# One weight load for two half-height matmuls: the Gram matrices of a cross-covariance attention kernel

## The chip, the cores and the metric

The kernel runs on one NeuronCore of a Trainium2 chip. The metric is the device time of one execution in microseconds (us), the median of several runs. A second number is used for reading: the span, which is the time from the first to the last instruction in one profiled execution.

## The reference

For each of 8 x 12 = 96 heads, Q, K and V are 512 x 64 in float32. Q and K are normalised along the sequence, a 64 x 64 matrix of attention is made from them, and V is multiplied by it:

```python
Q_norm = Q / (np.linalg.norm(Q, axis=-2, keepdims=True) + 1e-10)
K_norm = K / (np.linalg.norm(K, axis=-2, keepdims=True) + 1e-10)
attn = np.einsum('bhnd,bhne->bhde', Q_norm, K_norm)
attn = np.exp(attn - np.max(attn, axis=-1, keepdims=True))
attn = attn / (np.sum(attn, axis=-1, keepdims=True) + 1e-10)
return np.einsum('bhnd,bhde->bhne', V, attn)
```

## The kernel before

**Units.** Four heads make a unit u; there are U = 24 units. Two units make a step s (12 steps), two steps a window w of V (6 windows). In a unit's tiles each head lies on 32 partitions, and each partition holds T = 16 rows of 64 numbers. So partitions 0 to 63 hold heads 0 and 1, and partitions 64 to 127 hold heads 2 and 3.

**What a unit goes through.** Q and K arrive by DMA and are cast to bf16 into `qkb[u]`, K beside Q (`cast_qk`, on DVE, ACT or POOL). `mask_k` (L222, DVE) writes `km[u]`: K twice, side by side, once with the odd heads set to zero and once with the even heads set to zero. `square_q` (L228, ACT) squares Q. Then TensorE (PE) has four kinds of work and a fifth for V:

- `grams(u)` (L245): for each of 16 rows t and for each half g of the partitions, a matmul with 64 rows of `km` as weights (64 x 128) and the same 64 partitions of `qkb` as moving data (128 columns, K and Q). It accumulates K'K and K'Q of two heads in PSUM tile `gram`, each half g in a bank of its own. This makes 32 matmuls and 32 weight loads in a unit, 768 of each in all.
- `norms_q(u)` (L253): 8 matmuls with full-height weights and 4 columns of moving data, for the norms of Q.
- `logits(s)` (L300): two float32 transposes for a step.
- `vtrans` (L327): transposes of V, in groups of 8 (4 at the end), full-height weights.
- `outs(s, x)` (L343): 16 matmuls with weights of 128 x 32, the product of V and attention.

Between them stand `squares`, `cross`, `halves_q`, `sums`, `powers`, `scale_k`, `exps` and `normalise` (DVE, ACT, POOL) for the softmax, and the copies out of PSUM, `vcopy` and `ocopy`. Results leave by DMA on the queue of SP.

**What sets the order.** The order on each engine is written out by a planner (class `Order`): every piece of work has costs on its engines, pieces that it must follow and a rank, and a list simulation gives each engine's sequence. `grams` has a cost of 1.8 us for the first eight units and 1.2 us after; `size` counts PE instructions of a piece (64 for a `grams`), and `pause` stands for the fetching of PE's code. None of these numbers is changed. `km` and `qkb` have two buffers each, so that the casts of unit u + 2 wait for the Gram matmuls of unit u. PE executes in the order written, so that whatever stands behind a `grams` waits for it.

The profile calls a weight load LDWEIGHTS, on a row of its own, PEld. It names PE's instructions with the rows and columns of the array that they use: 64\*128 for the Gram matmuls and their loads, 128\*128 for `norms_q`, `logits` and `vtrans`, 128\*32 for `outs`.

## Time and profile before

| | |
|---|---|
| median of 3 runs | 127.69 us (127.62 to 127.79) |
| span of the profiled execution | 125.9 us |
| the profiled execution's own time | not listed beside its span; median less span is 1.8 us |
| mean granted clock of TensorE | 0.870 of full speed |
| PE busy / PEld busy | 79.6 us / 63.9 us |
| DVE / ACT / POOL busy | 98.8 / 91.0 / 50.0 us |
| moved by DMA | 50.63 MB, mean 402 GB/s |
| Gram matmuls (L245) | 768, mean 252 ns, 33.3 us busy |
| Gram weight loads (L245) | 768, mean 113 ns, 28.3 us busy |

Matmuls and loads are pipelined, so that the ends in the records are modelled, and records of neighbours overlap: 768 matmuls of 252 ns take 33.3 us and not 194. The starts are events. "Idle before, releaser" gives the time that an engine stood idle ahead of a group of instructions, and who ended that idleness.

### The profile page before, as it was taken

How to read it: one execution, taken by the hardware profiler on the slowest of the kernel's cores; microseconds unless marked ns; L12 is line 12 of the kernel's file. 1: busy time of each engine (PE TensorE's matmuls, PEld its weight loads, DVE VectorE, ACT ScalarE, POOL GpSimd, SP SyncE). 2: the span in 40 equal slices, each digit the busy share in tenths (PEclk: the TensorE clock that was granted, in tenths of full speed). 3: DMA queues.
4: the chain of work that ended last, by engine and by line, in shares of the span. 5: the costliest groups of instructions: out<-in, count | busy, mean ns of one | idle time of the engine just before them, and what ended most of it. 6: DMA issues, size and time to landing. Idle time of an engine off the chain costs nothing.

```text
span 125.9 us, 4630 instructions
## 1 busy us (share of the span) xinstructions
PE 79.6 (63%) x1944; PEld 63.9 (51%) x1944; DVE 98.8 (78%) x198; ACT 91.0 (72%) x217; POOL 50.0 (40%) x68
## 2 busy tenths in 40 slices
PE   0036949258789857766776668676794875976000
PEld 0035848236668745555665555555683764754000
DVE  3189676967959399987999989999979999999200
ACT  4243476579979999499999999999499997670000
POOL 6243353384561836633437226138743551000000
PEclk9999999955555899999999999999779999599555
DMA  3999999999999999999999999999999999999993
GB/s 105 401 419 419 422 414 418 432 424 410 439 409 418 414 433 414 410 431 419 411 428 428 403 419 423 424 424 407 426 413 420 410 415 407 417 411 404 400 411 134
DMA packets 12159, 50.63 MB, mean 402 GB/s; under 512 B 1130, under 2 KB 1130, under 8 KB 10730
## 3 DMA queue, kind: packets, MB, share of 16 engines
q1 hardware_dynamic: 11850, 49.29, 95.9%
q10 hardware_dynamic: 288, 1.05, 2.1%
q8 instruction: 15, 0.25, 0.7%
q14 instruction: 6, 0.05, 0.1%
HBM read 37.75 MB, written 12.58 MB: 400 GB/s over the span
## 4 chain that ended last, share of the span: by engine, by line
DVE 32%; ACT 24%; DMA 18%; PE 8%; issue 7%; POOL 3%; ACTq 0%; SPq 0%; POOLq 0%
DMA out_dram<-so 12%; DVE so L174 12%; DVE km L222 10%; DMA qk<-in_K_dram 6%; PE gram L245 6%; ACT vt L172 5%; ACT q L228 5%; ACT qkb L172 4%; ACT ex L307 4%; DVE ab L316 4%; DVE qkb L174 3%; ACT vb L172 2%; ACT kq L172 2%; POOL vb L176 2%; DVE n L280 1%
## 5 line engine op out<-in xcount | busy, mean ns | idle before, releaser
L245 PE MATMUL gram<-qkb,km 64*128 64x128 bf16 x768 | 33.3, 252 | 23.3 <-DVE km L222 23.3
L245 PEld LDWEIGHTS <-km 64*128 64x128 bf16 x768 | 28.3, 113 | 26.7 <-DVE km L222 26.3
L176 POOL TENSOR_SCALAR qkb<-qk 128x1024 bf16<-128x1024 f32 x24 | 25.4, 1062 | 28.6 <-PE gram L245 19.9
L222 DVE TENSOR_SCALAR km<-qkb,pick 128x1024 bf16<-128x1024 bf16 x48 | 30.3, 671 | 3.0 <-ACT qkb L172 2.4
L174 DVE COPY so<-po 128x512 f32<-128x512 f32 x48 | 30.8, 684 | 0.4
L228 ACT ACTIVATE q<-qk 128x1024 bf16<-128x1024 f32 x24 | 25.5, 1065 | 6.3 <-DMA qk<-in_Q_dram 4.3
L343 PE MATMUL po<-ab,vt 128*32 128x128 bf16 x768 | 20.1, 231 | 9.5 <-DVE so L174 6.9
L172 ACT COPY vt<-vps 128x1024 bf16<-128x1024 bf16 (+1 forms) x26 | 24.5, 956 | 1.2 <-PE vps L327 1.0
L343 PEld LDWEIGHTS <-vt 128*32 128x32 bf16 x768 | 13.4, 100 | 14.9 <-issue 10.7
L327 PE MATMUL vps<-identb,vb 128*128 128x128 bf16 x192 | 16.7, 237 | 3.0 <-ACT vt L172 2.2
L176 POOL TENSOR_SCALAR vb<-v 128x1024 bf16<-128x1024 f32 x13 | 15.0, 1156 | 8.4 <-DMA v<-in_V_dram 8.2
L307 ACT ACTIVATE ex<-lg,r 128x64 f32<-128x64 f32 x48 | 14.5, 325 | 1.6 <-PE lg L300 1.6
L327 PEld LDWEIGHTS <-vb 128*128 128x128 bf16 x192 | 12.6, 106 | 6.0 <-issue 3.1
L174 DVE CAST qkb<-qk 128x1024 bf16<-128x1024 f32 x13 | 12.1, 933 | 4.2 <-DMA qk<-in_K_dram 4.1
L293 POOL TENSOR_TENSOR kqs<-kq,r 128x256 f32<-128x256 f32 x12 | 7.9, 660 | 18.8 <-ACT r L289 8.3
L316 DVE TENSOR_TENSOR ab<-ex,rinv 64x256 bf16<-64x256 f32 x24 | 12.1, 504 | 0.6
L260 DVE SCALAR_TENSOR_TENSOR scr<-gram,eye 128x256 f32<-128x256 f32 x12 | 5.1, 424 | 8.5 <-ACT kq L172 5.7
L172 ACT CAST vb<-v 128x1024 bf16<-128x1024 f32 x11 | 11.7, 1062 | 0.0
L172 ACT CAST qkb<-qk 128x1024 bf16<-128x1024 f32 x11 | 11.6, 1054 | 0.0
L307 ACT ACTIVATION_READ_ACCUMULATOR ex<-lg,r 128x1 f32 x48 | 10.4, 217 | 0.0
L172 ACT COPY kq<-gram 128x256 f32<-128x256 f32 x12 | 4.6, 380 | 7.1 <-PE gram L253 3.1
L253 PEld LDWEIGHTS <-q 128*128 128x128 bf16 x192 | 7.5, 100 | 3.7 <-issue 2.7
(25 smaller groups left out, 41.1 us busy)
## 6 DMA issues: line engine op xcount, KB each, us to landing
out_dram<-so SPq DMA_DIRECT2D x23, 512.0 KB, 9.8
v<-in_V_dram SPq DMA_DIRECT2D x11, 1024.0 KB, 15.8
qk<-in_Q_dram SPq DMA_DIRECT2D x8, 1024.0 KB, 15.9
qk<-in_K_dram SPq DMA_DIRECT2D x8, 1024.0 KB, 17.6
qk<-in_Q_dram SPq DMA_DIRECT2D x8, 512.0 KB, 8.7
qk<-in_K_dram SPq DMA_DIRECT2D x6, 512.0 KB, 9.6
qk<-in_K_dram ACTq DMA_DIRECT2D x2, 512.0 KB
v<-in_V_dram SPq DMA_DIRECT2D x2, 512.0 KB
```

The lines of the kernel that those rows point to most:

```text
L172: nc.scalar.copy(o, i)
L174: nc.vector.tensor_copy(o, i)
L176: nc.gpsimd.tensor_scalar(out=o, in0=i, scalar1=1.0, scalar2=0.0, op0=ALU.mult, op1=ALU.add)
L222: nc.vector.tensor_scalar(out=km[u][:, :, a], in0=qkb[u][:, :, 0], scalar1=pick[:, a:a + 1], scalar2=None, op0=ALU.mult)
L228: nc.scalar.activation(q2[u], qk32[s][:, 0, r], AF.Square)
L245: nc.tensor.matmul(gram[s][:, 2 * g + r, 0:2 * D], km[u][rows, t].rearrange("p a d -> p (a d)"), qkb[u][rows, t].rearrange("p x d -> p (x ...
L253: nc.tensor.matmul(gram[s][:, 0, 2 * D + HU * r:2 * D + HU * (r + 1)], q2[u][:, 2 * t:2 * t + 2].rearrange("p t d -> p (t d)"), heads, sta ...
L293: (nc.vector if eng == "DVE" else nc.gpsimd).tensor_tensor(out=kqs[s], in0=kq[s], in1=r8[s][:, 0:HU, None].to_broadcast([128, 4, D]), op=A ...
L307: nc.scalar.activation(e[:, h, :], lg[s][:, h, :], AF.Exp, scale=r8[s][:, HU + h:HU + h + 1], accum_out=z[:, h:h + 1])
L316: nc.vector.tensor_tensor(out=a[half, :, half], in0=e[half], in1=ri[half, :, None].to_broadcast([D, HU, D]), op=ALU.mult,)
L327: nc.tensor.transpose(ps[:, c, n, :], vb[w][:, J * c + j].rearrange("p r d -> p (r d)"), identb)
L343: nc.tensor.matmul(po[s, x][32 * h:32 * (h + 1), j].rearrange("p r d -> p (r d)"), v, ab[s][:, h, :])
```

## The change

In `grams`, the two matmuls of a row t, one for each half of the partitions, no longer bring a weight load each. One load takes all 128 partitions of `km[u][:, t]`. Two matmuls follow, written by the new helper `stay` as bare matmul instructions that bring no load; each has the array tile of 64 rows and 128 columns at row 0 or row 64, the same moving data and the same place in PSUM as before. So a unit has 16 loads in the place of 32, and 32 matmuls as before. Nothing else is changed, the planner's numbers included.

```diff
+    def stay(o, w, i, size, at, start, stop):
+
+        low = nc.tensor.lower_ap
+        nc.tensor.add_instruction(mybir.InstMatmult(
+            name=nc.get_next_instruction_name(), engine=mybir.EngineType.PE, ins=[low(i), low(w)], outs=[low(o)],
+            start_tensor_calc=start, stop_tensor_calc=stop, tile_size=size, tile_position=at, ldweights=False))
+
...
         for t in range(T):
+            w = km[u][:, t].rearrange("p a d -> p (a d)")
+            nc.tensor.ldweights(w)
             for g in range(2):
                 rows = slice(64 * g, 64 * (g + 1))
-                nc.tensor.matmul(
-                    gram[s][:, 2 * g + r, 0:2 * D], km[u][rows, t].rearrange("p a d -> p (a d)"), qkb[u][rows, t].rearrange("p x d -> p (x d)"),
-                    start=(t == 0), stop=(t == T - 1))
+                stay(gram[s][:, 2 * g + r, 0:2 * D], w[rows], qkb[u][rows, t].rearrange("p x d -> p (x d)"),
+                     (64, 128), (64 * g, 0), t == 0, t == T - 1)
```

## The prediction

> **What bounds the kernel now.** I read the page first: busy shares, the 40 slices, the DMA queues.

> ```profile
> PE 79.6 (63%) x1944; PEld 63.9 (51%) x1944; DVE 98.8 (78%) x198; ACT 91.0 (72%) x217; POOL 50.0 (40%) x68
> PEclk9999999955555899999999999999779999599555
> DMA  3999999999999999999999999999999999999993
> q1 hardware_dynamic: 11850, 49.29, 95.9%
> L245 PE MATMUL gram<-qkb,km 64*128 64x128 bf16 x768 | 33.3, 252 | 23.3 <-DVE km L222 23.3
> ```

> The DMA engines are busy in every slice but the first and the last; the kernel is bound by its transfers. PE waits for data: 23.3 us ahead of the Gram matmuls, 8.3 of them at the start. So cheaper Gram matmuls can give next to nothing, and the question is whether they become dearer. From the first Gram matmul to the last PE has 8.3 to 101.0 us, 92.7 us for 24 units, or 3.87 us a unit.

> Next, the timeline of PE and of its loads, at full clock:

> ```profile
> 54.28 1.07 PE L245 MATMUL gram<-qkb,km 64*128 64x128 bf16 x32 [0.78 <-DVE km L222]
> 55.27 0.41 PE L343 MATMUL po<-ab,vt 128*32 128x128 bf16 x16
> 55.61 0.62 PE L327 MATMUL vps<-identb,vb 128*128 128x128 bf16 x8
> 54.27 0.90 PEld L245 LDWEIGHTS <-km 64*128 64x128 bf16 x32 [0.86 <-DVE km L222]
> 55.27 0.23 PEld L343 LDWEIGHTS <-vt 128*32 128x32 bf16 x16
> 55.61 0.45 PEld L327 LDWEIGHTS <-vb 128*128 128x128 bf16 x8
> 56.02 0.30 PEld L253 LDWEIGHTS <-q 128*128 128x128 bf16 x8
> ```

> Two readings. First, the pair: the last of 32 matmuls starts 1.07 - 0.216 = 0.854 us after the first, so 16 pairs follow each other every 56 ns, the two of a pair 3 ns apart by their starts. The 8 full-height transposes do the same: (0.62 - 0.219)/7 = 57 ns each with a load each. So 128 columns set the pace, and the loads lie beside them.

> Second, the seams. The last Gram matmul starts at 54.28 + 0.854 = 55.13; the first load of `outs`, another array shape, starts at 55.27, 0.14 us later. By single records every change of shape behind a 128-column matmul costs at least 144 to 148 ns, or 236 to 243 at half clock; no load ever starts sooner. Where the shape stays (transposes to `norms_q`, both 128\*128), the last transpose starts at 55.61 + 0.62 - 0.219 = 56.01 and the next load at 56.02: 1 to 2 ns later by single records. Behind the 4-column matmuls of `norms_q` a change costs 92 to 94 ns. [...]

> [...]

> **The change, part by part.**

> Removed: 384 of 768 loads. Their pace, (0.90 - 0.094)/31 = 26 ns, lies under the matmuls: worth 0. PE's code shrinks too: 0.25 MB in 15 instruction packets for 3888 matmuls and loads is 64 bytes each, so 24.6 KB of 50.63 MB go, 0.05% of the traffic. Idle of PE put down to "issue" ahead of matmuls is 0.4 us in all. I take 0 for both.

> Added: two changes of shape in every row t. The load is 128\*128, the two matmuls are 64\*128. Ahead of each load but a unit's first, PE empties from two 128-column matmuls: 144 ns (239 at half clock), measured. From the load to its first matmul of another shape no row exists. Lower bound: 3 ns, the distance without a change (54.27 to 54.28). Upper bound: the load's whole record, 94 ns at full and 148 at half clock, close to the 93 ns behind the shortest matmul. Matmuls are released 72 ns before their modelled end (216 - 144, 164 - 92); for a load at half clock that would be 148 - 73 = 75. I take the middle of 75 and 148, 110 ns at half clock, and 60 at full.

> A row t is then load to matmul + 3 ns + emptying: at full clock 0.060 + 0.003 + 0.144 = 0.207 us (0.150 to 0.241), at half clock 0.110 + 0.003 + 0.239 = 0.352 (0.245 to 0.390). Sixteen: 3.3 us (2.4 to 3.9) or 5.6 us (3.9 to 6.2), in place of 1.0 or 1.8. Behind the waiting load, PE's queue holds `norms_q`, transposes, `outs` and `logits`; for these wait POOL's casts (19.9 us behind the Gram matmuls already), the copies on ACT and DVE and, through them, the stores.

> **Which clock.** The windows of PE, cut where the granted clock changes:

> ```profile
> 31.60:35.00 3.40, 2.65 (x39) 0.50 1.02 425
> 35.00:38.40 3.40, 2.98 (x47) 0.50 1.03 420
> 38.40:41.90 3.50, 3.48 (x62) 0.50 1.02 415
> 86.20:89.70 3.50, 1.84 (x70) 0.99 1.00 411
> 93.10:96.50 3.40, 1.90 (x52) 1.00 1.01 416
> 113.50:117.00 3.50, 2.17 (x91) 0.99 1.02 398
> ```

> [...] I count, in each window, the share of time in which columns stream (53 ns at full, 107 at half clock for 128 columns, a pair or a foursome counted once). In the half-clock windows at 31.6 and 35.0 it is 0.72 and 0.60, and the clock stays; at 38.4 it is 0.79, and it rises. At full clock 0.41 (93.1) keeps it; 0.36 (86.2) and 0.35 (113.5) lose it. Busy time does not order them: 2.17 of 3.50 loses, 1.90 of 3.40 keeps. Work starts at half clock: the first Gram matmuls have records of 308 to 312 ns. In the changed Gram stage the share is 107/352 = 0.30 at half and 53/207 = 0.26 at full clock. [...] So I expect half clock until the Gram stage is over.

> **The sum.** PE's other work up to 101.0 us, counted from its rows with the seams, at half clock: 24 `norms_q` x 0.37, 19 groups of transposes x 1.04, 10 `logits` x 0.6, 30 `outs` x 0.57 = 51.8 us (29 at full clock, with 0.27, 0.50, 0.28 and 0.34). PE becomes the bound:

> 8.3 (start) + 24 x 5.63 + 51.8 + 3 (idle, an estimate; 25 now) + 22 (behind the last Gram matmul; 24.9 now, less since the stores no longer queue) = 220 us of span. With the 1.8 us between span and median: 222 us. With the load's bounds: 181 to 237.

> **Rivals.**

> *Drained, but at full clock.* 8.3 + 24 x 3.3 + 29 + 6 + 22 + 1.8 = 147 us; 134 to 157 over the bounds (at the lower one PE has hardly more work than time, and half its idle stays). It decides if emptying counts as activity. For it: PE is never idle then. Against it: the order of the windows above.

> [...]

> *No drain: not slower.* If only a load's shape against the last load's counts, or the load is issued as two of 64 rows, the row t stays at 56 ns, and transfers bound as before: 127.7 us, 127.2 to 128.2. From the point at which a row costs under some 80 ns (0.4 us more a unit, within PE's idle) nothing shows. For it: in every seam of the trace both the loads' and the matmuls' shapes change, so the two aren't told apart. Against it: it is the load that is held back there, with matmuls of another shape in flight, and that is what each row t now has. A little gain could come from fewer code fetches, a little loss from another rhythm of the DMA.

> **How the numbers follow.** Drained at half clock: 0.68. Drained at full or mixed clock: 0.16. No drain: 0.16, half of it faster, a quarter each way of the rest. A difference of about 0.2% (0.25 us) is what measurement can tell. So faster 0.08, same 0.04, slower 0.88. The likeliest case gives 222 us, 181 to 237 by its bounds; for 8 in 10 the range must reach into the full-clock case: 140 to 241.

> **What would show it.** Right: 384 loads of 128\*128 on `km`, each some 0.24 us behind the last matmul's start at half clock; Gram matmul busy above 100 us; mean granted clock near 0.55; DMA no longer full in the slices; PE's idle ahead of L245 near its first 8.3 us. Wrong: a Gram unit of 1.07 us still (no drain), or 3.3 us at a clock near 1. A row t of 0.245 us at half clock would mean that the load is not drained.

## The result, and the profile after

The changed kernel takes 210.91 us (210.33 to 212.68, 4 runs) where the kernel before takes 127.74 us: 1.6536 times as long, 95% interval 1.6466 to 1.6606. The forecast was 222 us, 140 to 241. The profiled execution took 210.54 us with a span of 208.7 us, 1.8 us outside the span as before. Ratios here and below compare only the runs of a kernel that lie within 1.5% of its fastest; medians and ranges are over all its runs.

The page of the changed kernel (busy time and instructions of each engine, slices of clock and DMA, the transfer queue, three groups of costliest instructions; the lines are now L215 for the bare matmul in `stay` and L251 for the explicit load):

```profile
PE 165.8 (79%) x1944; PEld 124.3 (60%) x2328; DVE 92.7 (44%) x198; ACT 93.2 (45%) x217; POOL 49.6 (24%) x68
PEclk9999999999999999999999975567555555557975
DMA  6999999708919509938609909980059940005686
q1 hardware_dynamic: 11850, 49.29, 62.4%
L215 PE MATMUL gram<-qkb,km 64*128 64x128 bf16 x768 | 109.0, 280 | 29.6 <-DVE km L229 9.7
L251 PEld LDWEIGHTS <-km 128*128 128x128 bf16 x384 | 40.3, 105 | 53.2 <-DVE km L229 12.8
L215 PEld LDWEIGHTS <-km 64*128 64x128 bf16 x768 | 40.2, 100 | 5.1 <-issue 0.2
```

Three things stand there. The DMA slices are full of holes: transfers no longer bound. The Gram matmuls, as many as before, are busy for 109.0 us in place of 33.3. And the loads did not become fewer: 2328 in place of 1944. The 768 loads of 64 rows are all still there, now under the line of the bare matmul, with 384 loads of 128 rows beside them. The change does not do what it says; every bare matmul still brings a load.

The timeline of the loads, first in a stretch at half clock, then in one at full clock (start, duration, operation, count):

```profile
99.47 0.10 PEld L251 LDWEIGHTS <-km 128*128 128x128 bf16 x1
99.58 0.11 PEld L215 LDWEIGHTS <-km 64*128 64x128 bf16 x2
99.80 0.10 PEld L251 LDWEIGHTS <-km 128*128 128x128 bf16 x1
99.92 0.10 PEld L215 LDWEIGHTS <-km 64*128 64x128 bf16 x2
...
117.07 0.10 PEld L251 LDWEIGHTS <-km 128*128 128x128 bf16 x1
117.18 0.10 PEld L215 LDWEIGHTS <-km 64*128 64x128 bf16 x2
117.34 0.10 PEld L251 LDWEIGHTS <-km 128*128 128x128 bf16 x1
```

A row t begins with the large load. The small loads, and with them the matmuls (4 to 5 ns later by single records), start 0.12 us behind it at half clock and 0.11 at full; the next large load comes 0.22 or 0.16 us after those. By single records: 117 + 7 + 214 = 338 ns at half clock, 107 + 8 + 155 = 270 at full (the 7 or 8 ns run from the first small load to the second matmul), where a row took 107 or 56 ns before. So each row has two waits at a change of shape: 117 or 107 ns from the large load to the small ones, and 214 or 155 ns from the second matmul to the next large load.

The waits for PE have grown to match (who waited for whom, us in all, times, longest; the first line is of the kernel before, where the Gram matmuls are L245):

```profile
POOL qkb L176 <- PE gram L245: 19.9, 10, 3.2
...
POOL qkb L176 <- PE gram L215: 64.7, 11, 10.4
DVE scr L268 <- PE gram L215: 27.5, 5, 6.9
```

POOL's casts waited 19.9 us for the Gram matmuls before, and wait 64.7 now.

**The clock.** The clock row holds a 9 up to 116 us, but this is not a reading: the first record of the clock in this execution is a rise to full speed at 115.9 us, and up to there nearly all rows take 335 to 340 ns, as in the stretches recorded at 0.50. So the page's mean of 0.827 is too high: with 0.50 up to 115.9 us it is 0.55. The same holds for the 0.870 of the kernel before, whose first record is a rise at 21.4 us while its rows up to there take 107 ns; it becomes 0.785. Of the 360 distances between two large loads inside a unit, 325 are at half clock (335 to 340 ns) and 26 at full (268 to 270); three lie at a change of the clock (280 to 330), and six are longer (459 to 570).

### The profile page after: what moved, and what is told of

It is laid out like the page before. It is cut to its first block, busy times and chain, and to the rows that moved or that the text cites. A ratio compares the mean times of both kernels' runs of the same rounds, so it can differ in the third digit from the quotient of the medians.

```text
span 208.7 us, 5011 instructions
## 1 busy us (share of the span) xinstructions
PE 165.8 (79%) x1944; PEld 124.3 (60%) x2328; DVE 92.7 (44%) x198; ACT 93.2 (45%) x217; POOL 49.6 (24%) x68
## 3 DMA queue, kind: packets, MB, share of 16 engines
q1 hardware_dynamic: 11850, 49.29, 62.4%
## 4 chain that ended last, share of the span: by engine, by line
PE 55%; issue 15%; PEld 12%; DVE 10%; ACT 2%; DMA 2%; POOL 1%; POOLq 0%; ACTq 0%; DVEq 0%
PE gram L215 37%; PE vps L335 8%; PE po L351 7%; PEld L215 5%; PEld L251 5%; DVE so L174 4%; DVE km L229 3%; DMA qk<-in_K_dram 2%; ACT vt L172 2%; PE gram L261 1%; PE lg L308 1%; DVE ab L324 1%; DVE qkb L174 1%; PEld L261 1%; POOL qkb L176 1%
## 5 line engine op out<-in xcount | busy, mean ns | idle before, releaser
L215 PE MATMUL gram<-qkb,km 64*128 64x128 bf16 x768 | 109.0, 280 | 29.6 <-DVE km L229 9.7
L251 PEld LDWEIGHTS <-km 128*128 128x128 bf16 x384 | 40.3, 105 | 53.2 <-DVE km L229 12.8
L176 POOL TENSOR_SCALAR qkb<-qk 128x1024 bf16<-128x1024 f32 x24 | 26.0, 1083 | 105.6 <-PE gram L215 64.7
L215 PEld LDWEIGHTS <-km 64*128 64x128 bf16 x768 | 40.2, 100 | 5.1 <-issue 0.2
L351 PE MATMUL po<-ab,vt 128*32 128x128 bf16 x768 | 25.3, 283 | 4.6 <-DVE so L174 3.0
L229 DVE TENSOR_SCALAR km<-qkb,pick 128x1024 bf16<-128x1024 bf16 x48 | 25.4, 571 | 6.7 <-ACT qkb L172 6.1
L335 PE MATMUL vps<-identb,vb 128*128 128x128 bf16 x192 | 22.5, 291 | 0.6 <-ACT vt L172 0.6
L351 PEld LDWEIGHTS <-vt 128*32 128x32 bf16 x768 | 16.7, 122 | 10.5 <-issue 7.2
L335 PEld LDWEIGHTS <-vb 128*128 128x128 bf16 x192 | 17.3, 132 | 3.8 <-issue 2.9
L172 ACT COPY kq<-gram 128x256 f32<-128x256 f32 x12 | 4.5, 376 | 31.6 <-DVE scr L268 12.2
L315 ACT ACTIVATE ex<-lg,r 128x64 f32<-128x64 f32 x48 | 14.5, 320 | 8.6 <-PE lg L308 8.6
L174 DVE CAST qkb<-qk 128x1024 bf16<-128x1024 f32 x13 | 10.8, 831 | 8.7 <-DMA qk<-in_K_dram 3.9
L324 DVE TENSOR_TENSOR ab<-ex,rinv 64x256 bf16<-64x256 f32 x24 | 11.3, 472 | 0.6
```

The costliest lines, as they stand in the source:

```text
L172: nc.scalar.copy(o, i)
L174: nc.vector.tensor_copy(o, i)
L176: nc.gpsimd.tensor_scalar(out=o, in0=i, scalar1=1.0, scalar2=0.0, op0=ALU.mult, op1=ALU.add)
L215: nc.tensor.add_instruction(mybir.InstMatmult(name=nc.get_next_instruction_name(), engine=mybir.EngineType.PE, ins=[low(i), low(w)], outs= ...
L229: nc.vector.tensor_scalar(out=km[u][:, :, a], in0=qkb[u][:, :, 0], scalar1=pick[:, a:a + 1], scalar2=None, op0=ALU.mult)
L251: nc.tensor.ldweights(w)
```

## The experiments

The theory (theory 1 in the expectations): the price is of the changes of array shape, two in each row, and of the half clock that goes with rows in which columns stream for a small share of the time (107 of 338 ns). The rivals: the bare matmul itself; an additional load, whatever its shape; the signals that each row now sends (one with each explicit load and one with its second matmul, where a unit sent one before); and, of the clock, that the changes of shape lower it as such, whatever is streamed between.

**The bare matmuls alone.**

```diff
-            nc.tensor.ldweights(w)
```

> The bare matmuls of the helper stay, without the explicit load of 128 partitions; the changed kernel's trace shows that each bare matmul has a 64*128 load of its own again, so this should be the kernel before in another spelling. Theory 1 (the cost is the two changes of array shape that the 128*128 load brings into each row): 127.7 us, within 0.3%, PE with 768 Gram loads and 56 ns a row at full clock. Rival 2 (the bare matmul itself, with its own dependencies and signals, breaks the pipeline): near 211 us, or at least far above 130.

Measured: 127.64 us, 0.9981 times the kernel before (0.9956 to 1.0005). 768 Gram loads, 33.5 us of Gram busy time. The helper is the old matmul in another spelling; all of the 83 us come with the explicit load.

**An extra load of the matmuls' own shape.**

```diff
-            nc.tensor.ldweights(w)
+            nc.tensor.ldweights(w[0:64], tile_position=(0, 0))
```

> The extra load stays in every row, 384 in all, but takes only the lower 64 partitions in the shape of the matmuls (64*128). Theory 1 (change of shape): no emptying; three loads a row of some 26 ns are 78 ns in place of 56 ns, which is 0.35 us a unit at full clock and nothing at half clock, within PE's idle: 127.5 to 129.5 us. Rival 3 (an additional load into rows of the array that are at work must wait for them, whatever its shape): at least 140 ns a row, 160 to 211 us.

Measured: 128.38 us (127.52 to 130.01, 10 runs), ratio 1.0018 (0.9982 to 1.0053): no difference that can be told. A Gram unit in the timeline of PE, from an execution of 129.89 us:

```profile
49.88 1.13 PE L215 MATMUL gram<-qkb,km 64*128 64x128 bf16 x32 [0.90 <-DVE km L229]
```

1.13 us in place of 1.07: by single records a row still takes 55 to 58 ns, but its two matmuls start 34 to 59 ns apart instead of 3, so that the unit ends 0.06 us later. So three loads fit beside a pair of matmuls, 384 more loads cost nothing that can be told, and the two signals a row, which this kernel sends too, cost nothing either. My 78 ns a row was too dear: its 26 ns a load was the pace of loads that come two to a pair of matmuls of 56 ns, and here they follow each other every 19 ns on average.

**The large loads, but in one bunch.**

```diff
-            nc.tensor.ldweights(w)                      # in each row of grams
+        for t in range(T):                              # ahead of norms_q's own loads
+            nc.tensor.ldweights(km[u][:, t].rearrange("p a d -> p (a d)"))
```

> The 16 extra loads of 128 partitions of each unit are kept, but stand together ahead of norms_q, whose own loads are 128*128 too, and not between the rows. Same instructions as in the changed kernel, 24 changes of shape fewer than 24 x 32 by far. Theory 1: 16 x 25 to 30 ns = 0.4 to 0.5 us more on PE in a unit, within its idle: 127.7 to 130 us. Rival 4 (the price is of the 384 loads themselves or of their signals, 3.4 us a unit): near 211 us.

Measured: 132.89 us, ratio 1.0384 (1.0337 to 1.0431): above what theory 1 expected, and far from 211. The loads' timeline in one unit:

```profile
57.22 0.45 PEld L336 LDWEIGHTS <-vb 128*128 128x128 bf16 x8
57.63 0.70 PEld L260 LDWEIGHTS <-km 128*128 128x128 bf16 x16
```

Sixteen loads with no matmul between them take 0.70 us, (0.70 - 0.1)/15 = 40 ns each, and not the 25 to 30 that I took from loads with matmuls; at half clock they take 47 to 50 ns. By their starts that is 15.6 us more on PE in all 24 units. The time between the first and the last Gram unit for which neither a matmul nor a load is on record shrank by 10.3 us, from 24.8 to 14.5, and the last Gram unit ended at 106.0 us where it had ended at 100.8, about the 5.2 us of the result. The same 384 loads of the same shape as in the changed kernel thus cost 5 us where they bring few changes of shape, and 83 where they bring 32 a unit.

**Every second row.**

```diff
-            nc.tensor.ldweights(w)
+            if t % 2 == 0:
+                nc.tensor.ldweights(w)
```

> The load of 128 partitions only in every second row, 192 in all. Row times measured in the changed kernel: 107 + 4 + 155 ns at full clock and 117 + 7 + 214 at half clock for a row with the load, 56 and 104 for a row without. Two rows: 322 or 442 ns; a Gram unit 2.6 or 3.5 us. Theory 1 with the clock decided by the share of time in which columns stream: the Gram stage streams 0.47 at half clock, too little to rise (0.73 and more did), so half clock and 8.3 + 24 x 3.54 + 51.8 + 3 + 22 + 1.8 = 172 us. If the clock were full: 130 to 135 us. A cost in proportion to the number of loads with no account of the clock: 127.7 + 83.2/2 = 169 us.

Measured: 164.27 us (160.64 to 165.42, 4 runs). This lies under both 172 and 169 and does not tell them apart: a badly chosen dose. The rows cost what was expected: two of them took 441 to 446 ns at half clock (442 expected) and 324 to 326 at full (322). The clock was mixed, and not at half throughout: its records, which begin at 87.8 us, hold three stretches at full speed.

**Every fourth row.** The same edit with `t % 4 == 0`.

> The load of 128 partitions in every fourth row, 96 in all. Four rows: 107 + 4 + 3 x 56 + 155 = 434 ns at full, 117 + 7 + 3 x 104 + 214 = 650 ns at half clock; a Gram unit 1.74 or 2.6 us in place of 1.0 or 1.8. At half clock the Gram stage is 24 x 2.6 + 51.8 = 114 us and the whole 150 us; at full clock PE has idle left and the transfers bound, 128 to 130 us. Theory 1 with the clock by streaming: the Gram rows stream 0.64 at half and 0.49 at full clock, so it rises sooner and holds: 132 to 142 us. In proportion to the loads: 127.7 + 83.2/4 = 148.5 us.

Measured: 137.87 us, ratio 1.0757 (1.0672 to 1.0843). This does tell: a price in proportion to the number of loads, 148.5 us, is out. Four rows took 655 to 660 ns at half clock (650 expected; a pair adds 107 ns there, and not 104) and 435 to 438 at full (434). With a quarter of the loads PE's idle takes up a part of the price (the time with no matmul or load on record fell from 24.8 to 14.2 us), and the clock is at full speed for most of the span behind 54.7 us.

**Another shape within the same half.**

```diff
-            nc.tensor.ldweights(w)
+            nc.tensor.ldweights(w[0:64, 0:D], tile_position=(0, 0))
```

> The extra load of each row takes the lower 64 partitions and 64 columns only, the shape 64*64, beside matmuls of 64*128. It needs no row of the array that the 64*128 load of the experiment with 128.4 us did not need. Theory 1 (any change of shape empties PE): the rows cost as in the changed kernel, 337 ns at half clock, and the time is 205 to 215 us. Rival 5 (a load over both halves of the array must wait for the matmuls in both, and nothing else): 127.5 to 129.5 us.

Measured: 217.93 us, ratio 1.7027 (1.6926 to 1.7127), a little above the 205 to 215 expected. The group of the extra loads:

```profile
L251 PEld LDWEIGHTS <-km 64*64 64x64 bf16 x384 | 46.9, 122 | 54.5 <-DVE km L229 11.0 <-issue 1.2 <-DVE ab L324 0.3
```

A load that is smaller than the free one of 128.38 us, in the same rows and in half of its columns, costs 90 us: a row takes 353 ns at half clock, 15 more than in the changed kernel. So the wait is not for the other half of the array or for rows at work. In these two runs, 128.38 us against 217.93, it goes with the change of shape, here of the columns alone.

**Three pairs in each row.**

```diff
+            for n in range(3):
                 for g in range(2):
...
-                     (64, 128), (64 * g, 0), t == 0, t == T - 1)
+                         (64, 128), (64 * g, 0), t == 0 and n == 0, t == T - 1 and n == 2)
...
-        nc.gpsimd.memset(heads[32 * h:32 * (h + 1), h:h + 1], 1.0)
+        nc.gpsimd.memset(heads[32 * h:32 * (h + 1), h:h + 1], 3.0)
```

> The changed kernel with each row's pair of Gram matmuls issued three times, 2304 in the place of 768, and the ones of the norms' constant set to 3, which leaves the quotient as it was. Row: 107 + 4 + 2 x 56 + 155 = 378 ns at full, 117 + 7 + 2 x 104 + 214 = 546 ns at half clock. Theory 1 with the clock by streaming: the Gram rows stream 0.44 at full clock (0.39 and more held it), so once up it stays up: 8.3 + 24 x 6.05 + 29 + 3 + 22 + 1.8 = 209 us plus what the start at half clock costs, 210 to 235 us, about the time of the changed kernel with a third of the matmuls. Rival 6 (emptying the array lowers the clock whatever is streamed between): half clock throughout, 8.3 + 24 x 8.74 + 51.8 + 3 + 22 + 1.8 = 297 us.

Measured: 280.62 us (270.75 to 287.73, 4 runs): my 210 to 235 is wrong by far, and 297 is nearer. The windows of an execution of 270.75 us (length, busy of PE, PEld, DVE, ACT, POOL, granted clock, DMA share, GB/s) show why it is nevertheless not the rival's case:

```profile
190.60:228.10 37.50, 31.18 (x664) 24.41 (x723) 18.94 (x38) 20.61 (x49) 9.70 (x10) 1.00 0.43 156
228.10:245.20 17.10, 15.73 (x196) 10.97 (x222) 2.27 (x6) 1.33 (x3) 1.62 (x2) 0.50 0.01 2
```

For 37.5 us the clock stood at full speed while Gram rows with two changes of shape went through, 380 ns each (378 expected); in the second window a row took 548 to 553 (546 expected). So two changes of shape in each row do not by themselves lower the clock, and the row prices hold in both. What failed was my account of how it rises and stays up: at half clock columns stream for 0.58 of a Gram row (three pairs of 107 ns in 548 to 553), below the 0.78 from which windows were followed by a rise in the traces of the two kernels (*The clock*, below), and the first recorded rise of the execution stands at 132.5 us; behind it the clock row of the page is below 9 in three stretches, slices 23 and 24, 26 to 29 and 35 to 37 of 40.

## Why the prediction was right, and where not

The range of 140 to 241 us took in both clocks. The mechanism is to be judged by its likeliest case, 222 us, which is 5% above the 210.91 measured.

*What bounds the kernel.* Right, as far as the runs go: a kernel with 384 Gram loads more (128.38 us) cannot be told from the kernel before, so the loads were not what bound it. One with fewer loads was not run. (PE's 92.7 us for 24 units are 3.86 us each, not 3.87.)

*"Removed: 384 of 768 loads."* Wrong. I took the diff at its word; the trace has 384 loads more, not fewer, and I had no rival for this. It cost the sum nothing, since 384 loads of 64 rows more or less could not be told in the time (128.38 us with them); that much was luck, for what was forecast was the price of a load shared by two matmuls, and what was measured is the price of a load nobody needs. A load that was really shared would be 128\*128 ahead of matmuls of 64\*128 as well; that each of its rows would hold the same two waits is an estimate from those measured here, 107 and 155 ns at full clock. It wasn't tried, since every matmul written so got its own load.

*Two changes of shape in each row.* Right, and shown by the experiments: without the load 127.64, with a load of the same shape 128.38, of another 210.91 or 217.93. The two kernels with an extra load in 64 rows differ in its columns alone: 128.38 us with the matmuls' shape, 217.93 with 64\*64. What the prediction calls emptying or draining is a wait in the traces: in the kernel before, at full clock, the load of another shape starts 144 to 148 ns behind the start of the last 128-column matmul, and a load of the same shape 1 to 2 ns behind it. What PE does in that time no trace shows.

*The price of a row.* At half clock 352 ns forecast, 338 measured: the load's part a little too cheap (110 against 117), the matmuls' part too dear (239 against 214). The 239 ns came from matmuls at the end of a stream; behind a lone pair the wait is 25 ns shorter. At full clock it is longer instead, 155 ns behind a lone pair against 144 to 148, and why the two clocks differ in this is open. The forecast of 207 ns at full clock was too low and its upper bound of 241 too: 270 measured, as the wait behind the load takes 107 ns where I allowed at most its record of 94. The full-clock rival's 147 us rested on this and was too low as well: with 270 ns a row the same sum gives 171 us. By that estimate the waits cost some 43 of the 83 us and the half clock the other 40.

*The clock.* Right for this kernel: 325 of 360 rows at half clock. Windows of the changed kernel (length, busy of PE, granted clock, DMA share, GB/s):

```profile
136.40:139.80 3.40, 3.40 (x75) 0.51 0.92 319
139.80:143.20 3.40, 2.58 (x44) 1.00 0.19 71
143.20:190.00 46.80, 41.02 (x452) 0.50 0.36 131
```

*The sum,* from the starts in the changed kernel's trace:

| term | forecast, us | measured, us |
|---|---|---|
| up to the first Gram load | 8.3 | 8.2 |
| 24 Gram units | 135.2 | 128.4 |
| PE's other work up to the last Gram unit | 51.8 | 45.0 |
| idle of PE between | 3 | 3.2 |
| behind the last Gram unit | 22 | 23.8 |
| span | 220 | 208.7 |

The two terms that are off, 6.8 us each, carry the difference; 1.8 us behind the last unit go the other way. Of the second, transposes were 16.1 us where I had 19.8, and `logits` 3.9 where I had 6.0, because I priced pieces with a seam behind each, and several stand ahead of a piece of the same shape.

*What would show it.* DMA slices no longer full and Gram busy above 100 us came as named. The mean clock near 0.55 came too, once the stretch without records is put at half clock; the page's own 0.827 hides it. One sign was misread in advance: PE's idle ahead of the Gram matmuls, 29.6 us and not near 8.3, since the wait ahead of each pair (107 or 117 ns behind the large load) is counted there too; 9.7 us of it are put down to data. The large load stood 0.21 us behind the last matmul's start at half clock, where 0.24 was named.

## What to carry to other kernels

Before adding a weight load or a matmul of another tile shape between others, look in the timeline at what a change of shape costs (last start of one shape to the first load of the next), and multiply it by the number of changes, not by the number of instructions: 384 loads of the same shape could not be told from none here (128.38 us, ratio 1.0018), one of another shape cost 0.2 us in its row. Ask next for what share of the time columns still stream: in the changed kernel it was 107 of the 338 ns of a row at half clock, 325 of 360 rows ran at that clock, and it made a row a quarter longer (338 ns against 270). And count the instructions of the changed kernel in its profile before believing that the edit did what it says.

## What the runs showed of the hardware that I had not expected

- The wait at a change of shape stands behind a load too: behind one of 128\*128 the loads of 64\*128 start 107 ns later at full and 117 at half clock, almost the same, where behind a 128-column pair it is 155 and 214.
- Loads of 128\*128 back to back with no matmul between them take 40 ns each at full clock and 47 to 50 at half; three loads of 64\*128 beside a pair of matmuls fit into 55 to 58 ns.
- Three times the Gram matmuls in the rows of the changed kernel cost 110 ns a row more at full clock (380 against 270), about twice the 56 ns of a pair, so that the two waits together are as long with three pairs as with one.
